# Compressing the paged cache: the next unit's transposes issued inside this unit's matmuls

## The chip, the cores and the metric

The kernel runs as one program on one core of a Trainium2 chip. The metric is the device time of one execution in microseconds (us). Three executions of the kernel before took 2334.25, 2342.62 and 2344.47 us; the median, 2342.62 us, is the time before. A profile of a further execution is what the rows below come from.

## The reference

The reference is one inference step of a two-layer decoder for a prompt of 1024 tokens and for eight decode rows that each have 8192 past tokens in a paged cache. In each layer a normalised input is projected into the inputs of four head groups (sparse attention, a gated recurrence, pooling, attention on a memory), their outputs are gated and projected back. The part that matters here is the sparse attention's compressed keys and values of the decode rows:

```
def compress_rows(rows, pe, w1, w2):          # rows: 8192 cache rows of 64 numbers, keys or values
    blk = rows.reshape(B, n, 32, Hk, 64) + pe # blocks of 32 rows
    flat = blk ... reshape(B, n, Hk, 32 * 64) # 2048 numbers for each block
    return silu(flat @ w1) @ w2               # w1: 2048 x 256, w2: 256 x 64
```

It is done for the keys and for the values of all eight decode rows, 256 blocks each, in both layers; the compressed rows are then what the decode rows score to choose the blocks that they attend to.

## The kernel before

Each layer runs in four phases: A (norms, first projections), P2 (the rest of the projections, prompt attention), P3 (the recurrence, the decode rows' window and memory attention, and the compression of the cache, which is `stageC`), and O (output projection, and the decode rows' selection, which reads the compressed rows). The order of the instructions on each engine is fixed when the program is built: a planner goes through all instructions of a phase by priority and by its own estimate of when each can start, and puts on an engine the first one by priority that is ready by that estimate (L1797). Earlier code has the earlier priority; `stageC` has a later priority than all else in P3 (L1750), so that its matmuls fill what the recurrence and the attention (below: the other lane) leave of TensorE. On the chip every engine keeps that order, whatever the real durations are.

`stageC` (L450) works through 16 units; a unit is 128 blocks, half of a decode row's cache. For each unit:

- `cload` (L511) brings the unit's cache pages into four groups of tiles R (g = 0 to 3), each with two halves. One half comes by four direct DMAs, two issued by SP and two by ACT (L541), the other by two indirect DMAs issued by POOL (L524); one VectorE copy per half (L544) puts the values next to the keys. There are four slots for each half (`rb` is 4), so one unit's rows fill them all, and a group's load can start when the transposes of the group that was there are done.
- `ctrans` (L548) turns R into X, with the positions along the partitions: for each group and for t = 0 (keys) and t = 1 (values), four 128 x 128 transposes on TensorE (L246, tile `ct`) fill one PSUM bank, ACT copies the bank as the rounded part Xh (L564) and VectorE subtracts it for the remainder Xl (L565). The transposes turn through three PSUM banks, which the transposes of the hidden layer (`ct` from `xs`, in `csilu`) use too. X has three buffers for the two sets that a unit needs, so the next unit's key set goes into the free one, and its value set into the one that this unit's key product has done with.
- `cmm` (L568) makes the product with w1 for keys or for values: 16 steps q of three matmuls of 256 columns each (`mm3`, L118: Xh with w1's rounded part, Xh with its remainder, Xl with its rounded part), accumulated in one PSUM bank.
- `ctail` (L612) applies the SiLU and w2 to the unit before, and writes it out (L621, L622, SP).

The order before is: loads of unit u+1; all 48 matmuls of the key product of u; tail of u-1; all 32 transposes of u+1, group by group, keys and values in turn; the 48 matmuls of the value product of u.

Of the kernel before, what the change touches and what calls it, by code (L numbers as in the profile page):

```python
# [9 lines left out]
F32 = mybir.dt.float32  # L10
F32R = mybir.dt.float32r
# [101 lines left out]
class Net:  # L113
# [336 lines left out]
    def stageC(self, l, cp, rb):  # L450

        nc = self.nc
        xp, self.cxp, self.cxn = cp["s"], [cp[f"X{n}"] for n in range(3)], 0
        R = [self.cload(l, 0, g, cp["R"], rb) for g in range(4)]
        W = self.cweights(l, cp)
        X = self.ctrans(R)
        hid = None
        for u in range(16):
            yield u
            R = [self.cload(l, u + 1, g, cp["R"], rb) for g in range(4)] if u < 15 else None  # L460
            new = [self.cmm(X[0], W, 0)]
            if u:
                self.ctail(l, u - 1, hid, W, xp)
            if R:
                nx = self.ctrans(R)
            new.append(self.cmm(X[1], W, 1))
            hid, X = new, nx
        self.ctail(l, 15, hid, W, xp)

    def cpe(self, l, wp):  # L470
# [74 lines left out]
            parts += [(R[:, pr, c1 - 1:c1 + 1], R[:, pr, c1 + 1:c1 + 3]) for pr in range(2)]  # L545
        return parts

    def ctrans(self, Rs):  # L548
        nc = self.nc
        X = []  # L550
        for t in range(2):
            n = self.cxn % 3
            self.cxn += 1
            pool = self.cxp[n]
            X.append([pool.tile([128, 16, 128], F32R, name=f"X{p}{n}", bufs=1) for p in "hl"])
        for g, R in enumerate(Rs):
            for t in range(2):
                ps = self.psT()
                for pr in range(4):
                    self.tr(ps[:, pr * 128:pr * 128 + 128], R[pr][t].rearrange("p s d -> p (s d)"))  # L560
                pv = ps.rearrange("p (b r) -> p r b", r=16)
                hi = X[t][0][:, :, g * 32:g * 32 + 32]
                lo = X[t][1][:, :, g * 32:g * 32 + 32]
                nc.scalar.copy(hi, pv)  # L564
                nc.vector.tensor_tensor(lo, pv, hi.bitcast(F32), op=OP.subtract)  # L565
        return X

    def cmm(self, X, W, t):  # L568
        ps = self.lane("h")
        for q in range(16):  # L570
            w = W[0][t][q // 8]
            self.mm3(ps[:, :256], X[0][:, q], X[1][:, q], w[0][:, q % 8], w[1][:, q % 8], q == 0, q == 15)
        return ps

    def csilu(self, hid, n, bB, xp):

# [1224 lines left out]
```

## Time and profile before

| | |
|---|---|
| median of three executions | 2342.62 us (2334.25 to 2344.47) |
| profiled execution | 2343.6 us |
| span of its instructions | 2341.8 us |
| TensorE matmul busy | 2048.5 us, 87% |
| VectorE, ACT, POOL busy | 65%, 38%, 32% |
| mean granted clock of TensorE | 0.93 |

The profiled execution's time is its span and 1.8 us around it. Times in the rows are microseconds from the start of the span, unless ns is written. PE is TensorE's matmuls and PEld its weight loads, DVE is VectorE, SPq and ACTq are the issues of DMAs. `ct`, `ch` and `R` are tile names; "L246 PE MATMUL ct<-cst,R" is the transposes of R, "ch<-w1h,Xh" a product with w1. A matmul's duration in a row runs past the start of the next one, since matmuls overlap; what one costs is the distance between two starts.

### The profile page before, as it was taken

The numbers are of one execution on the slowest core, as the hardware profiler recorded it, in microseconds if no ns is written. First come the engines' busy times: TensorE is split into PE (matmuls) and PEld (weight loads), VectorE is DVE, ScalarE is ACT, GpSimd is POOL, SyncE is SP. The second block draws the span as 40 slices with busy tenths as digits, with TensorE's granted clock in tenths as the row PEclk, the third lists the DMA queues.
The fourth block names the chain that finished last, engine by engine and source line by source line (L and its number), as shares of the span: only waits on it lengthen the run. The fifth ranks groups of instructions, "written<-read, shape, count | busy, mean of one in ns | idle before, by whom it ended". The sixth has DMA issues, their size and how long they took to land.

```text
span 2341.8 us, 41952 instructions
## 1 busy us (share of the span) xinstructions
PE 2048.5 (87%) x14396; PEld 1824.7 (78%) x14396; DVE 1511.6 (65%) x3927; ACT 888.2 (38%) x2221; POOL 746.7 (32%) x841
## 2 busy tenths in 40 slices
PE   4999998894798999896979999898949899998878
PEld 4997888784788888785669979887838888878645
DVE  7874377885777666553298724788867776656523
ACT  4223366553433323230152234675545333333101
POOL 2002123313655543223020012243146555532340
PEclk8999999997899899898989999999969998998889
DMA  7237321106655446776253363221086544467661
GB/s 249 92 109 184 94 78 52 58 26 169 176 146 149 119 125 184 201 235 200 87 171 105 112 155 98 66 61 47 28 208 170 140 135 136 138 190 221 174 206 51
DMA packets 324093, 312.97 MB, mean 134 GB/s; under 512 B 60619, under 2 KB 285783, under 8 KB 323608
## 3 DMA queue, kind: packets, MB, share of 16 engines
q1 hardware_dynamic: 261544, 213.25, 31.1%
q0 software_dynamic: 24320, 79.71, 11.7%
q10 hardware_dynamic: 38016, 17.32, 2.8%
q8 instruction: 115, 1.88, 0.3%
q14 instruction: 98, 0.80, 0.1%
HBM read 255.00 MB, written 59.57 MB: 134 GB/s over the span
## 4 chain that ended last, share of the span: by engine, by line
PE 58%; DVE 16%; DMA 11%; issue 8%; ACT 3%; POOL 2%; SPq 2%; ACTq 0%; DVEq 0%; another core or an unknown queue 0%; POOLq 0%
PE ch L120 3%; PE ch L122 3%; PE mt L246 3%; PE ct L246 3%; PE ch L121 3%; PE aa L121 3%; PE aa L122 3%; PE aa L120 3%; PE mt L1429 2%; PE oa L122 2%; PE oa L120 2%; PE oa L121 2%; DVE P L804 2%; PE fa L120 2%; PE fa L122 2%
## 5 line engine op out<-in xcount | busy, mean ns | idle before, releaser
L524 POOL DMA_INDIRECT R<-in_cache_nsa_dram,idxc x256 | 253.1, 989 | 295.8 <-PE ct L246 192.5
L120 PE MATMUL ch<-w1h,Xh 128*128 128x256 f32 x1024 | 314.3, 307 | 17.6 <-ACT Xh L564 8.7
L122 PE MATMUL ch<-w1h,Xl 128*128 128x256 f32 x1024 | 311.4, 304 | 6.1 <-DVE Xl L565 3.2
L121 PE MATMUL ch<-w1l,Xh 128*128 128x256 f32 x1024 | 308.7, 301 | 0.4 <-issue 0.4
L120 PEld LDWEIGHTS ch<-w1h,Xh 128*128 128x128 f32 x1024 | 209.1, 204 | 23.5 <-ACT Xh L564 10.2
L122 PEld LDWEIGHTS ch<-w1h,Xl 128*128 128x128 f32 x1024 | 208.4, 204 | 13.8 <-DVE Xl L565 5.7
L148 POOL TENSOR_TENSOR wl<-wf,wh 128x1024 fp32r<-128x1024 f32 (+2 forms) x42 | 94.9, 2271 | 377.1 <-ACT wh L139 295.6
L564 ACT CAST Xh<-ct 128x512 fp32r<-128x512 f32 x256 | 146.0, 585 | 180.0 <-PE ct L246 109.9
L121 PEld LDWEIGHTS ch<-w1l,Xh 128*128 128x128 f32 x1024 | 209.0, 204 | 2.0 <-issue 0.4
L565 DVE TENSOR_TENSOR Xl<-ct,Xh 128x512 fp32r<-128x512 f32 x256 | 172.4, 683 | 42.8 <-ACT Xh L564 26.1
L246 PE MATMUL ct<-cst,R 128*128 128x128 f32 x1024 | 163.9, 292 | 40.7 <-DVE Xl L565 31.0
L246 PEld LDWEIGHTS ct<-cst,R 128*128 128x128 f32 x1024 | 122.1, 149 | 53.2 <-DVE Xl L565 33.7
L544 DVE COPY R<-R 128x256 f32<-128x256 f32 x260 | 92.5, 370 | 107.5 <-DMA R<-in_cache_nsa_dram,idxc 68.9
L121 PE MATMUL aa<-wl,hTh 128*128 128x326 f32 (+1 forms) x512 | 156.6, 307 | 5.1 <-POOL wl L148 5.1
L120 PE MATMUL aa<-wh,hTh 128*128 128x326 f32 (+1 forms) x512 | 156.4, 307 | 4.0 <-ACT wh L139 4.0
L122 PE MATMUL aa<-wh,hTl 128*128 128x326 f32 (+1 forms) x512 | 156.1, 305 | 0.0
L447 ACT ACTIVATE P<-ms,nst 128x512 f32<-128x512 f32 (+3 forms) x192 | 106.6, 557 | 78.7 <-DVE nst L777 78.0
L120 PE MATMUL fa<-hTh,wh 128*128 128x344 f32 x384 | 129.4, 337 | 4.2 <-ACT fo L381 3.9
L122 PE MATMUL fa<-hTh,wl 128*128 128x344 f32 x384 | 125.1, 326 | 0.0
L121 PE MATMUL fa<-hTl,wh 128*128 128x344 f32 x384 | 125.1, 326 | 0.0
L820 DVE TENSOR_TENSOR pl<-mt,ph 128x512 fp32r<-128x512 f32 (+1 forms) x160 | 101.2, 644 | 33.9 <-ACT ph L819 29.0
L777 DVE TENSOR_REDUCE nst<-ms 128x1 f32<-128x512 f32 (+3 forms) x192 | 98.0, 517 | 32.4 <-PE ms L774 19.2
(558 smaller groups left out, 5722.9 us busy)
## 6 DMA issues: line engine op xcount, KB each, us to landing
wf<-in_w_in_dram SPq DMA_DIRECT2D x34, 512.0 KB
R<-in_cache_nsa_dram SPq DMA_DIRECT2D x256, 64.0 KB
R<-in_cache_nsa_dram ACTq DMA_DIRECT2D x256, 64.0 KB
zd<-fo SPq DMA_DIRECT2D x48, 172.0 KB
pwf<-in_cmp_w_dram SPq DMA_DIRECT2D x32, 256.0 KB
wof<-in_w_out_dram SPq DMA_DIRECT2D x16, 512.0 KB
oo<-od SPq DMA_DIRECT2D x16, 512.0 KB
oz<-zd SPq DMA_DIRECT2D x16, 512.0 KB
```

The lines of the kernel that those rows point to most:

```text
L120: mm(out, lh, rh, start=first, stop=False)
L121: mm(out, lh, rl, start=False, stop=False)
L122: mm(out, ll, rh, start=False, stop=last)
L148: e.tensor_tensor(lo, src, hi.bitcast(F32), op=OP.subtract)
L246: self.nc.tensor.transpose(out, in_, self.ident[:in_.shape[0], :in_.shape[0]])
L447: self.nc.scalar.activation(out, S, AF.Exp, bias=nm, accum_out=sm)
L524: nc.gpsimd.indirect_dma_start(R[:, j].rearrange("p c d -> p (c d)"), None, rows, bass.IndirectOffsetOnAxis(ap=self.idxc[:, l, at + j:at + ...
L544: nc.vector.tensor_copy(Rs[:, :, :, 2], R[:, :, 0:2])
L564: nc.scalar.copy(hi, pv)
L565: nc.vector.tensor_tensor(lo, pv, hi.bitcast(F32), op=OP.subtract)
L777: nc.vector.tensor_reduce(one(nm), S, axis=AX.X, op=OP.max, negate=True)
L820: nc.vector.tensor_tensor(pl[:, :n], ps[:, :n], ph[:, :n].bitcast(F32), op=OP.subtract)
```

## The change

The value and key transposes of unit u+1 are no longer one block between the two products of unit u. Each product's loop over q issues the four transposes of one group after steps q = 1, 5, 9 and 13: in the key product those of the keys of u+1, in the value product those of its values. The loads start one unit earlier in the code (unit 1 is loaded before the loop), and the load of group g of unit u+2 stands right behind the value transposes of group g of u+1, in the value product of u. The number of loads, transposes, matmuls, copies and subtracts is the same, and so are the buffers.

```diff
-        R = [self.cload(l, 0, g, cp["R"], rb) for g in range(4)]
+        load = lambda u, g: self.cload(l, u, g, cp["R"], rb)
+        R = [load(0, g) for g in range(4)]
         W = self.cweights(l, cp)
-        X = self.ctrans(R)
+        X = [self.cX() for _ in range(2)]
+        for g in range(4):
+            for t in range(2):
+                self.ctrans(R[g], g, t, X[t])
+        R = [load(1, g) for g in range(4)]
         hid = None
         for u in range(16):
             yield u
-            R = [self.cload(l, u + 1, g, cp["R"], rb) for g in range(4)] if u < 15 else None
-            new = [self.cmm(X[0], W, 0)]
-            if u:
-                self.ctail(l, u - 1, hid, W, xp)
-            if R:
-                nx = self.ctrans(R)
-            new.append(self.cmm(X[1], W, 1))
-            hid, X = new, nx
+
+            new, nx, nR = [], [], []
+            for t in range(2):
+                if u < 15:
+                    nx.append(self.cX())
+                ps = self.lane("h")
+                for q in range(16):
+                    self.cmm(ps, X[t], W, t, q)
+                    if q % 4 == 1 and u < 15:
+                        self.ctrans(R[q // 4], q // 4, t, nx[t])
+                        if t and u < 14:
+                            nR.append(load(u + 2, q // 4))
+                new.append(ps)
+                if t == 0 and u:
+                    self.ctail(l, u - 1, hid, W, xp)
+            hid, X, R = new, nx, nR
...
-    def ctrans(self, Rs):
...
+    def cX(self):
+        n = self.cxn % 3
+        self.cxn += 1
+        return [self.cxp[n].tile([128, 16, 128], F32R, name=f"X{p}{n}", bufs=1) for p in "hl"]
+
+    def ctrans(self, R, g, t, X):
+
+        nc = self.nc
+        ps = self.psT()
+        for pr in range(4):
+            self.tr(ps[:, pr * 128:pr * 128 + 128], R[pr][t].rearrange("p s d -> p (s d)"))
+        pv = ps.rearrange("p (b r) -> p r b", r=16)
+        hi = X[0][:, :, g * 32:g * 32 + 32]
+        lo = X[1][:, :, g * 32:g * 32 + 32]
+        nc.scalar.copy(hi, pv)
+        nc.vector.tensor_tensor(lo, pv, hi.bitcast(F32), op=OP.subtract)
+
+    def cmm(self, ps, X, W, t, q):
+        w = W[0][t][q // 8]
+        self.mm3(ps[:, :256], X[0][:, q], X[1][:, q], w[0][:, q % 8], w[1][:, q % 8], q == 0, q == 15)
```

## Rows read from the trace of the kernel before

**Rows 1.** The profile's page: engines' busy time, and the drains of the transposes.
```profile
PE 2048.5 (87%) x14396; PEld 1824.7 (78%) x14396; DVE 1511.6 (65%) x3927; ACT 888.2 (38%) x2221; POOL 746.7 (32%) x841
L564 ACT CAST Xh<-ct 128x512 fp32r<-128x512 f32 x256 | 146.0, 585 | 180.0 <-PE ct L246 109.9
L565 DVE TENSOR_TENSOR Xl<-ct,Xh 128x512 fp32r<-128x512 f32 x256 | 172.4, 683 | 42.8 <-ACT Xh L564 26.1
```

**Rows 2.** Stage C by layer: PE, PEld, DVE, ACT, POOL busy; clock, DMA share, GB/s.
```profile
598.00:1048.00 450.00, 413.16 (x3412) 374.46 (x3411) 292.42 (x744) 153.08 (x403) 202.62 (x280) 0.93 0.58 166
1750.00:2195.00 445.00, 402.96 (x3361) 367.38 (x3360) 302.13 (x746) 161.97 (x410) 217.96 (x282) 0.91 0.58 163
```

**Rows 3.** Waits of TensorE in layer 0's stretch: total us, times, longest.
```profile
PE ct L246 <- DVE Xl L565: 10.2, 7, 3.6
PE ch L122 <- DVE Xl L565: 3.2, 4, 1.6
PE ch L122 <- DVE R L544: 1.6, 1, 1.6
```

**Rows 4.** The same in layer 1's stretch.
```profile
PE ct L246 <- DVE Xl L565: 9.7, 8, 3.2
PE ch L120 <- ACT Xh L564: 8.7, 3, 6.2
```

**Rows 5.** TensorE in order of time: eight and four transposes among products.
```profile
721.17 1.09 PE L246 MATMUL ct<-cst,R 128*128 128x128 f32 x8
...
722.22 0.28 PE L120 MATMUL ch<-w1h,Xh 128*128 128x256 f32 x1
722.34 0.28 PE L121 MATMUL ch<-w1l,Xh 128*128 128x256 f32 x1
...
723.66 0.60 PE L246 MATMUL ct<-cst,R 128*128 128x128 f32 x4
...
724.21 0.28 PE L121 MATMUL ch<-w1l,Xh 128*128 128x256 f32 x1
```

**Rows 6.** One wait of the transposes, TensorE in order of time.
```profile
758.59 0.63 PE L246 MATMUL ct<-cst,R 128*128 128x128 f32 x4 [2.53 <-DVE Xl L565]
```

**Rows 7.** Busy time and clock just after that wait, and in a longer stretch.
```profile
760.70:767.50 6.80, 6.80 (x43) 6.21 (x44) 4.86 (x13) 1.02 (x3) 0.95 (x2) 0.50 0.55 155
832.40:955.20 122.80, 115.76 (x995) 103.03 (x993) 73.28 (x199) 38.17 (x92) 51.08 (x64) 1.00 0.59 170
```

**Rows 8.** One group's load: transposes that free it, POOL's issue, copies, next transposes.
```profile
776.63 1.06 PE L246 MATMUL ct<-cst,R 128*128 128x128 f32 x8
...
778.45 1.06 POOL L524 DMA_INDIRECT R<-in_cache_nsa_dram,idxc  x1 [0.15 <-issue]
...
784.60 0.53 DVE L544 COPY R<-R 128x256 f32<-128x256 f32 x2 [1.89 <-DMA R<-in_cache_nsa_dram,idxc]
...
809.06 0.62 PE L246 MATMUL ct<-cst,R 128*128 128x128 f32 x4
```

**Rows 9.** First and last product with w1 in each layer.
```profile
L120 PE MATMUL ch<-w1h,Xh x512: 274/283/584, 598.0 to 1020.2; 128*128 128x256 f32 x171
L120 PE MATMUL ch<-w1h,Xh x512: 276/283/582, 1755.1 to 2167.3; 128*128 128x256 f32 x171
```

**Rows 10.** SP's queue in order of time: two stretches of other loads before R's.
```profile
901.14 8.18 SPq L968 DMA_DIRECT2D W<-in_cache_nsa_win_dram  x8
910.11 5.91 SPq L541 DMA_DIRECT2D R<-in_cache_nsa_dram  x4
...
943.23 9.48 SPq L1183 DMA_DIRECT2D msV<-in_cache_mem_dram  x7
...
956.31 0.64 SPq L541 DMA_DIRECT2D R<-in_cache_nsa_dram  x2
```

**Rows 11.** VectorE's longest waits in layer 0's stretch: total us, times, longest.
```profile
DVE R L544 <- DMA R<-in_cache_nsa_dram,idxc: 39.3, 23, 6.4
```

More of the change, by code (lines that the diff above doesn't have):

```diff
@@ L546, in cload @@
         return parts
-    def ctrans(self, Rs):
-        nc = self.nc
[L550 to L573, printed above, removed]
+    def cX(self):
[3 more added lines that the diff above has]
+    def ctrans(self, R, g, t, X):
+        nc = self.nc
+        ps = self.psT()
[9 more added lines that the diff above has]
+        self.mm3(ps[:, :256], X[0][:, q], X[1][:, q], w[0][:, q % 8], w[1][:, q % 8], q == 0, q == 15)
     def csilu(self, hid, n, bB, xp):
```

## The prediction

> **What bounds the kernel now.** I read the busy times first, then the busy times by stretch, then TensorE's waits inside the two stretches that hold stage C, and last the queues that feed it. TensorE is busy 87% of the span and no other engine passes 65% [rows 1]. The change touches only stage C, so its stretches matter: 450 us in layer 0 and 445 us in layer 1 [rows 2]. In them TensorE is busy 413.2 and 403.0 us, that is 92% and 91%, VectorE 65 and 68%. The phase is bound by TensorE, and what a new order can give back is the rest: 36.8 + 42.0 = 78.8 us without a matmul, and what the lower clock takes. The mean granted clock is 0.93 and 0.91 there [rows 2]; since the clock has two levels, 2.4 and 1.2 GHz, the time at the lower one is 2 x 0.07 x 450 + 2 x 0.09 x 445 = 143 us, and work done in it would have taken half: at most 71 us.
>
> The waits tell whose fault the idle time is. Those that belong to the chain from the transposes to the products are transposes that wait for a bank until Xl is out of it (10.2 and 9.7 us), products that wait for Xl, for the copy in R, or for Xh (3.2, 1.6 and 8.7 us): 33.4 us together [rows 3, 4], 42% of the 78.8. The other 45 belong to the recurrence, the hidden layer's chain and the decode rows' attention, which the change leaves alone.
>
> **The transposes themselves: 0.** The number stays. Their cost among products is read from distances between starts [rows 5]: products alone stand 722.34 - 722.22 = 0.12 us apart; eight transposes and one product take 722.22 - 721.17 = 1.05, so the eight take 0.93; four and one product take 0.55, so the four take 0.43. A group of four is not dearer than half of an eight (0.465). A layer has 128 groups, both have 256; were all now in eights the change would gain 256 x 0.035 = 9 us; if each group of four paid a boundary of 0.08 (0.20 instead of 0.12 for the first product behind it, were it not already in the 0.43) for the half of the groups that are new, it would lose 10. I take 0: fours already stand among products in these very rows, because the planner lets value products in while a bank is not free. The change therefore spreads over the key product what is now woven into the value product only.
>
> **The waits for drains: -25.** Now a group is issued as soon as the planner thinks that its bank is free. The drain is ACT's 0.585 and VectorE's 0.683 behind it [rows 1], 1.27 us without the handing over, and anything else that holds VectorE goes straight into a wait of TensorE, as the 2.53 us of [rows 6]. After the change two groups are twelve products and four transposes apart, 12 x 0.12 + 0.43 = 1.87 us. With three banks a bank comes round after two whole distances and twelve products, 2 x 1.87 + 1.44 = 5.2 us, against 1.27: some 3.9 us in hand. The longest waits for Xl are 3.6 and 3.2 us [rows 3, 4], so most would go. So would the products' waits: the key set is complete half a unit before its product, and the value set has a whole key product between its last group and its own product. But the hidden layer's transposes take two turns of the same three banks in each unit, and the planner need not keep the even order that the code writes. Between 0 and -33.4 I take three quarters.
>
> **The clock: -11.** Behind the wait of [rows 6] the clock is 0.50 for 6.8 us with TensorE busy all through [rows 7]: 3.4 us lost for a gap of 2.5. If the 71 us were shared as the idle time is, 42% or 30 us would go with the 33.4; since part of the low time is itself idle, and other gaps next to the removed ones hold the clock down, I take half of three quarters of that. Bounds 0 and -30.
>
> **The loads: +10.** This is where the change takes something away. A slot of R is now freed by the value transposes and refilled long before it is wanted: the transposes that free one end at 777.7, POOL issues at 778.45, the copies end at 785.1, and the next transposes come at 809.06 [rows 8]. That is 7.4 us of load and 24 us in hand. After the change a group is held from its key transposes to its value transposes, half a unit later, and the load has the other half. A unit lasts (1020.2 - 598.0) / 16 = 26.4 us in layer 0 and 25.8 in layer 1 [rows 9], so the half is 13.2 and what is left in hand is 5.8 us. POOL's two issues per group fit, and so do ACT's. SP is the queue to look at: it issues two of a group's six DMAs and is at times taken by other loads for longer, 9.0 us from 901.14 to 910.11 and 13.1 from 943.23 to 956.31 [rows 10]; there are six such stretches, three in each layer (the recurrence's first loads, the window's, the memory's). Over 5.8 that leaves 3.2 and 7.3, on average 5.2, and a fall of the clock of 3.4 each: 6 x 8.6 = 51 us if nothing else covers it. What covers it are the products: with a group late, the rest of the key product, 48 x 0.12 = 5.8 us, and the value product can go first, if the planner has foreseen it. Bounds 0 and 51; I take a fifth, because the planner sees these loads stand in SP's queue and only misjudges how long they take.
>
> Here the Trainium skill speaks to a term. Its page "DMA: Bandwidth & Descriptors", section "Issuing engines are not separate DMA queues", says that issuing from several engines saves only the time on the sequencer, and that this time is usually small beside the transfer. By that rule SP's turn would not delay a load, the term would be nought and the sum 2307. The row disagrees: eight issues took SP 8.18 us [rows 10], more than a whole load of 7.4. I go by the row.
>
> **The rest: 0.** The prologue makes the same transposes and loads in the same order. At the end, unit 15's last group stands near the end of unit 14's value product, a few microseconds before R goes to the output phase, which has all of unit 15's products to wait for anyway. Give 5 us either way for a new order of the other lane, whose instructions still go first by priority.
>
> **Sum.** -25 - 11 + 10 = -26 on the profiled execution's 2343.6 us: 2317.6. That execution is 1.0 above the median of the runs, so on the median 2317 us.
>
> **Rivals.** First, that nothing much changes. The planner issues by readiness and had woven fours into the value products already [rows 5]; it may fill its own plan to the brim either way, and the waits come from what it misjudges, so that they turn up at other instructions. For it: 45 of the 78.8 us of idle time have nothing to do with transposes. Against it: the waits for Xl recur, fifteen times. Time 2343, within 8.
>
> Second, slower: the loads become the bound. The place is the key transposes of unit u+1 in the key product of u, the point is when load and queue together pass 13.2 us, and the price is the 51 us above. VectorE keeps its order too, and it waits 39.3 us for indirect loads in layer 0 already [rows 11]; a copy that waits longer holds up the Xl behind it, which takes half of the gain (36) away: 2343.6 + 51 - 18 = 2376, and between that and about 2352 if half of the six stretches bite. For it: 24 us in hand shrink to 5.8. Against it: that is still more than the usual lateness, 39.3 / 23 = 1.7 us.
>
> Third, slower: the clock. Products that alternate with transposes all through a unit change banks all the time and may stop for moments at each change; if the low time then doubled with the woven share, 143 us more at half rate cost 71, less the 25: 2390. Against it: 122.8 us in a row, with transposes among the value products in several units, ran at 1.00 [rows 7]. The Trainium skill has this as a rule: "TensorE: Matmul & The Clock Gate", section "A second HAM failure mode: psum-queue depth-cycling", tells of a kernel whose cycling through banks made TensorE idle for moments and its clock swing. By that rule the time is the 2390; the trace speaks against it.
>
> **Chances.** Forecast 0.50, with its own range 2298 to 2333; nothing changes 0.23; loads 0.21; clock 0.04; 0.02 for what I don't see. For the range I go down to 2290 (a third more than my gain, most of the bounds of the drain and clock terms) and up to 2364, the middle of the loads' case. What a measurement of this kernel can tell from no change is about 0.5%, 12 us. Faster by more holds nearly all of the forecast and a fifth of the first rival, 0.55; within it 0.21; slower 0.24.
>
> **What would show it.** Transposes of R in fours with about twelve products between them through the whole unit, in the key product too. Waits of transposes for Xl under 7 us in both layers together, waits of products for Xl and Xh near none; the mean clock 0.94 or more in both stretches; both stretches some 13 us shorter; from the end of a group's copies to its key transposes some 6 us instead of 24. I am wrong if transposes or copies of R wait for DMAs by tens of microseconds, if the key product is still solid, or if the stretches are shorter and the output phase gives it back.

## The result, and the profile after

The changed kernel takes 2397.8 us (2396.3 to 2400.0), the kernel before 2339.9 beside it: ratio 1.0249, 95% interval 1.0223 to 1.0276. It is slower, and outside the range that was given. Two later timings gave 1.0205 [1.0154, 1.0257] and 1.0225 [1.0202, 1.0249]. The kernel before itself took 2274 to 2276 us beside some of the experiments and 2340 to 2345 beside the others, so only ratios to it are compared.

The profiled execution took 2398.2 us (span 2396.3). First the page's busy times and drains, which answer to [rows 1], then the busy times of the two stretches [rows 2] and the first and last product of stage C in each layer [rows 9].

```profile
PE 2078.7 (87%) x14396; PEld 1845.2 (77%) x14396; DVE 1509.4 (63%) x3927; ACT 887.3 (37%) x2221; POOL 735.7 (31%) x841
L575 ACT CAST Xh<-ct 128x512 fp32r<-128x512 f32 x256 | 147.8, 584 | 336.9 <-PE ct L246 211.9
L576 DVE TENSOR_TENSOR Xl<-ct,Xh 128x512 fp32r<-128x512 f32 x256 | 173.8, 684 | 59.3 <-ACT Xh L575 45.0
```

```profile
598.00:1058.00 460.00, 408.93 (x3320) 369.95 (x3321) 275.07 (x726) 143.95 (x392) 203.66 (x280) 0.90 0.52 147
1780.00:2240.00 460.00, 406.66 (x3333) 368.12 (x3334) 289.54 (x741) 156.06 (x404) 207.13 (x282) 0.91 0.54 151
```

```profile
L120 PE MATMUL ch<-w1h,Xh x512: 274/283/582, 596.8 to 1051.0; 128*128 128x256 f32 x171
...
L120 PE MATMUL ch<-w1h,Xh x512: 277/283/581, 1784.9 to 2233.2; 128*128 128x256 f32 x171
```

The drains did not get dearer: they last 584 and 684 ns, as before. ScalarE waits longer for the transposes (211.9 us instead of 109.9). From its first to its last product stage C lasts 454.2 us instead of 422.2 and 448.3 instead of 412.2: 68 us more. Between the two stages stand 734 us instead of 735, and behind the second one 163.1 instead of 174.5. So stage C loses all of it, and the end gives 11 back. TensorE's records between first and last product, added up, split the 68: 32 us are time without a matmul (35.0 to 49.7 and 32.8 to 49.9), 24 are half of the longer busy time at the lower clock (148 us of it instead of 100), and 12 are more busy time at full clock. Only some 3 of these 12 are other work, 32 matmuls of the memory attention that came to lie inside layer 1's stage; the rest are longer distances between starts, 6 us of them at the first product of a step.

The clock fell in both layers. In layer 0 it went from 0.93 to 0.90. In layer 1 the two figures of 0.91, here and in [rows 2], hide it, because both stretches run past the last product. Between first and last product it is 0.93 before, in the first line, and 0.91 after, in the second:

```profile
1755.10:2167.30 412.20, 379.36 (x3261) 347.81 (x3260) 279.91 (x724) 150.18 (x393) 196.65 (x268) 0.93 0.57 162
1784.90:2233.20 448.30, 398.36 (x3294) 362.28 (x3295) 278.58 (x726) 147.80 (x393) 204.10 (x281) 0.91 0.53 147
```

What TensorE waits for, layer 0's stretch and then layer 1's, answers to [rows 3, 4]: total us, times, longest.

```profile
PE ct L246 <- DVE R L557: 12.4, 8, 4.5
...
PE ct L246 <- issue: 7.8, 3, 5.3
...
PE ct L246 <- DVE Xl L576: 2.9, 4, 1.0
```

```profile
PE ct L246 <- issue: 13.2, 6, 5.3
PE ct L246 <- DVE Xl L576: 8.9, 9, 3.3
PE ct L246 <- DVE R L557: 7.5, 3, 5.5
```

The waits for drains are indeed smaller. Of the 33.4 us that the prediction priced, 27.8 lie between first and last product, and 7.0 of these are left, 3.2 in layer 0 and 3.8 in layer 1. The other 5.6 stand in the prologue of layer 1, which the change leaves alone, as do 5.1 of the 8.9 in layer 1's rows. The transposes now wait for the copies inside the loaded rows R, which they never did between first and last product before. Most of what is listed as "issue" there is the same wait: in front of each of the longest ones a copy of R ended 0.10 us before. With these it is 20 us in layer 0 and 19 in layer 1.

The next rows follow one group of the changed kernel as [rows 8] do before: the value transposes that free the slot, POOL's and SP's issues, the last copy, the key transposes, the value transposes.

```profile
899.64 0.60 PE L246 MATMUL ct<-cst,R 128*128 128x128 f32 x4
...
903.66 0.95 POOL L537 DMA_INDIRECT R<-in_cache_nsa_dram,idxc  x1 [0.30 <-issue]
...
906.65 3.12 SPq L554 DMA_DIRECT2D R<-in_cache_nsa_dram  x3
...
911.48 0.29 DVE L557 COPY R<-R 128x256 f32<-128x256 f32 x1 [0.82 <-DMA R<-in_cache_nsa_dram]
...
911.83 1.11 PE L246 MATMUL ct<-cst,R 128*128 128x128 f32 x4 [0.58 <-DVE R L557]
...
924.28 0.60 PE L246 MATMUL ct<-cst,R 128*128 128x128 f32 x4
```

The slot is free at 900.2 and the copy ends at 911.8, 11.5 us instead of 7.4; TensorE takes the keys as soon as they are there, and the values 12.4 us later. The same four distances, taken over the 56 groups of a layer that are loaded inside the loop (us, layer 0 / layer 1; "late" counts groups whose copy ended under 1.5 us ahead of their transposes, with an error of two or three because copies can change places):

```
                          slot free to copied  copied to keys  keys to values  late of 56
kernel before                  10.3 / 10.3       14.9 / 14.4      1.6 /  1.7     0 /  0
change                         12.0 / 12.1        2.5 /  2.6     14.9 / 14.3    23 / 18
values only                     9.3 /  9.8       16.3 / 14.8      1.4 /  1.4     0 /  0
half hold                      11.7 / 11.8        2.8 /  2.6     13.3 / 12.2    21 / 25
five slots                     11.4 / 10.9       10.3 / 10.6     12.4 / 13.0     5 /  3
four slots, same cuts           9.7 / 10.4        4.8 /  4.4     12.7 / 13.5     9 /  8
five slots, other cuts         10.1 / 11.0        7.1 /  7.2     14.6 / 14.0    10 /  8
four slots, other cuts         11.2 / 11.1        1.4 /  1.6     14.0 / 13.9    32 / 28
the same, timed again          12.0 / 11.7        2.1 /  2.1     13.3 / 13.1    25 / 21
```

The longest waits come where the memory attention's rows are loaded. SP's queue, ScalarE, VectorE and TensorE of the changed kernel in order of time, and then busy times in the 40 us from SP's burst on in both layers (columns as in [rows 2]):

```profile
951.45 8.52 SPq L1190 DMA_DIRECT2D msV<-in_cache_mem_dram  x7
...
952.70 1.07 ACT L575 CAST Xh<-ct 128x512 fp32r<-128x512 f32 x2 [2.52 <-PE ct L246]
...
956.00 0.70 DVE L557 COPY R<-R 128x256 f32<-128x256 f32 x2 [6.65 <-DMA R<-in_cache_nsa_dram,idxc]
...
956.80 1.08 PE L246 MATMUL ct<-cst,R 128*128 128x128 f32 x4 [5.26 <-issue]
...
957.09 1.27 DVE L576 TENSOR_TENSOR Xl<-ct,Xh 128x512 fp32r<-128x512 f32 x2
...
965.28 3.28 SPq L554 DMA_DIRECT2D R<-in_cache_nsa_dram  x3
...
970.04 1.09 PE L246 MATMUL ct<-cst,R 128*128 128x128 f32 x4 [4.49 <-DVE R L557]
```

```profile
951.00:991.00 40.00, 26.95 (x170) 25.20 (x169) 20.76 (x44) 7.69 (x17) 10.14 (x11) 0.74 0.74 232
2129.00:2169.00 40.00, 26.26 (x165) 23.85 (x163) 20.35 (x43) 6.79 (x17) 9.19 (x10) 0.74 0.76 232
```

And the kernel before, from its burst on:

```profile
943.00:983.00 40.00, 30.89 (x225) 28.38 (x225) 24.04 (x52) 11.63 (x26) 16.02 (x16) 0.87 0.90 260
2112.00:2152.00 40.00, 31.37 (x250) 29.88 (x248) 24.76 (x51) 12.00 (x28) 7.58 (x8) 0.87 0.65 193
```

335 matmuls instead of 475 fit into these 80 us. At the 3412 in 450 us of [rows 2] the missing 140 are worth an estimated 18 us: about a quarter of the 68. The rest is spread over other units, which last from 7 us less to 11 us more than before.

The same rows show what a copy does that VectorE reaches too early. ScalarE had copied two banks by 953.8, but VectorE stood for a load until 956.0 and subtracted the two banks only from 957.1 on: two finished drains waited 3.3 us behind a copy.

### The profile page after: what moved, and what is told of

Read it like the earlier page. It is cut to its first block, busy times and chain, and to the rows that moved or that the text cites. A ratio compares the mean times of both kernels' runs of the same rounds, so it can differ in the third digit from the quotient of the medians.

```text
span 2396.3 us, 41986 instructions
## 1 busy us (share of the span) xinstructions
PE 2078.7 (87%) x14396; PEld 1845.2 (77%) x14396; DVE 1509.4 (63%) x3927; ACT 887.3 (37%) x2221; POOL 735.7 (31%) x841
## 4 chain that ended last, share of the span: by engine, by line
PE 58%; DVE 14%; DMA 10%; issue 8%; ACT 4%; POOL 2%; SPq 2%; another core or an unknown queue 1%; ACTq 0%; DVEq 0%; POOLq 0%
PE ct L246 4%; PE ch L120 4%; PE ch L122 4%; PE ch L121 4%; PE mt L246 3%; PE aa L121 3%; PE aa L120 3%; PE aa L122 3%; PE mt L1436 3%; PE oa L121 2%; PE oa L122 2%; PE oa L120 2%; DVE P L811 2%; DMA R<-in_cache_nsa_dram 2%; PE fa L120 2%
## 5 line engine op out<-in xcount | busy, mean ns | idle before, releaser
L120 PE MATMUL ch<-w1h,Xh 128*128 128x256 f32 x1024 | 324.3, 317 | 6.8 <-issue 3.9
L575 ACT CAST Xh<-ct 128x512 fp32r<-128x512 f32 x256 | 147.8, 584 | 336.9 <-PE ct L246 211.9
L246 PE MATMUL ct<-cst,R 128*128 128x128 f32 x1024 | 185.3, 303 | 69.8 <-issue 23.9
L122 PEld LDWEIGHTS ch<-w1h,Xl 128*128 128x128 f32 x1024 | 212.1, 207 | 12.6 <-issue 10.3
L246 PEld LDWEIGHTS ct<-cst,R 128*128 128x128 f32 x1024 | 129.9, 154 | 83.8 <-issue 43.9
L557 DVE COPY R<-R 128x256 f32<-128x256 f32 x260 | 85.3, 345 | 90.5 <-DMA R<-in_cache_nsa_dram,idxc 54.2
```

The source lines that it names most:

```text
L120: mm(out, lh, rh, start=first, stop=False)
L122: mm(out, ll, rh, start=False, stop=last)
L246: self.nc.tensor.transpose(out, in_, self.ident[:in_.shape[0], :in_.shape[0]])
L557: nc.vector.tensor_copy(Rs[:, :, :, 2], R[:, :, 0:2])
```

## The experiments

Each is timed beside the kernel before. The cuts shown leave out lines, marked with dots, that only carry the edit through. The runs follow in the order in which they were made. The kernel before was at 2274 us beside the first four (values only to no loads) and at 2276 beside another four (from the cuts in the values-only order to the extra transposes), and at 2343 to 2345 beside all others.

**Values only.** All eight groups of a unit stand in the value product, the load right behind: the weave without the hold.

```diff
-                if u < 15:
-                    nx.append(self.cX())
+                if t and u < 15:
+                    nx = [self.cX() for _ in range(2)]
...
-                    if q % 4 == 1 and u < 15:
-                        self.ctrans(R[q // 4], q // 4, t, nx[t])
-                        if t and u < 14:
+                    if t and q % 4 == 1 and u < 15:
+                        for s in range(2):
+                            self.ctrans(R[q // 4], q // 4, s, nx[s])
+                        if u < 14:
```

> Both sets of transposes of a group stand in the value product, after steps 1, 5, 9 and 13, and the load right behind them: the groups are spread by hand as in the change, but a slot of R is held no longer than before. If the loss comes from slots held half a unit longer: the loads have some 24 us again, about 2340, between 2325 and 2350. If the spreading itself costs (clock, boundaries, a worse plan): most of the loss stays, 2370 to 2400.

Measured 2281.4 us, ratio 1.0022 [0.9998, 1.0046]. The loss is gone, and so are the waits for R; transposes wait for Xl again (17.2 us in layer 0). The change itself was not timed while the kernel before took 2274 us; the late-loads run below has this order too and gives 1.0036 where the change gives 1.0205.

**Half hold.** Key groups behind steps 8, 10, 12, 14 of the key product, value groups behind 0, 2, 4, 6 of the value product.

```diff
-                    if q % 4 == 1 and u < 15:
-                        self.ctrans(R[q // 4], q // 4, t, nx[t])
+                    g = q // 2 - (0 if t else 4)
+                    if q % 2 == 0 and 0 <= g < 4 and u < 15:
+                        self.ctrans(R[g], g, t, nx[t])
...
-                            nR.append(load(u + 2, q // 4))
+                            nR.append(load(u + 2, g))
```

> As the change, but the key transposes stand after steps 8, 10, 12 and 14 of the key product and the value transposes after steps 0, 2, 4 and 6 of the value product, so that a slot is held for 8 steps instead of 16: the load has three quarters of a unit, 20 us, 12 in hand instead of 6. If the hold is the cause: 2340 to 2360, at least half of the loss gone. If the weave is the cause, which is the same in number and denser: 2390 or more.

Measured 2308.6 us, ratio 1.0186 [1.0135, 1.0237]: a miss. But the table shows why: the planner placed the groups so that the slots were still held 13.3 and 12.2 us. The edit did not do what it was for.

**No loads.** The loads and copies of units 2 to 15 are left out, and unit 1's rows are used for all of them: in the change, whose edit is shown, and in the kernel before.

```diff
-                            nR.append(load(u + 2, q // 4))
+                            nR.append(R[q // 4])
```

> The change without the loads and copies of R for units 2 to 15 (unit 1's rows are used again, so the compressed rows are of the wrong units). If late loads are the cause, the change's order is no slower than the order before under the same cut: within 12 us of the next run, and both some 20 to 60 us below 2340. If the weave is the cause: 40 to 60 us above the next run.

> The kernel before with the same loads and copies left out (unit 1's rows are used again, so the compressed rows are of the wrong units): the partner of the run above. Both theories: 2290 to 2325, since the transposes' waits for drains stay and VectorE has 0.37 us less per copy to do.

Measured 2181.8 us, ratio 0.9589 [0.9569, 0.9609], and 2171.4 us, ratio 0.9547 [0.9531, 0.9563]. The distance of the two is within what was expected, their fall is not: 93 and 103 us below the 2274 beside them, where 20 to 60 and 15 to 50 below 2340 had been expected. Stage C's stretches, first of the change and then of the kernel before, both without loads:

```profile
590.00:956.00 366.00, 358.32 (x3293) 334.94 (x3292) 244.13 (x611) 145.58 (x389) 96.15 (x168) 0.98 0.22 65
1669.00:2040.00 371.00, 362.55 (x3303) 336.63 (x3304) 255.25 (x619) 157.45 (x399) 96.77 (x169) 0.98 0.24 66
```

```profile
593.00:964.00 371.00, 361.03 (x3311) 333.90 (x3310) 253.48 (x617) 145.55 (x396) 96.69 (x168) 0.99 0.24 69
1666.00:2040.00 374.00, 363.92 (x3315) 337.03 (x3314) 262.26 (x625) 154.01 (x403) 97.68 (x168) 0.98 0.24 69
```

Without loads TensorE is busy 97 to 98% in either order and its clock is 0.98 or 0.99. So the drains and banks, which the change was to relieve, cost next to nothing by themselves: the idle time and the low clock of stage C come with the loads and their copies, which this pair does not tell apart. The change is then even 4.4 and 2.3 us shorter inside stage C, but what follows each stage is 11 us longer, and in sum it is 10 us slower. Loads cost 4.5% in the old order.

**Late loads.** Values only, with the loads issued in the key product of the next unit.

```diff
+                    if t == 0 and q % 4 == 1 and 0 < u < 15:
+                        R.append(load(u + 1, q // 4))
...
-                        if u < 14:
-                            nR.append(load(u + 2, q // 4))
```

> The values-only order (all eight groups woven into the value product, ratio 1.002 before), but the loads of the next unit are issued in the key product, half a unit later than there, so a load has the same 13.2 us before its transposes as in the change, and nothing is held longer than in the kernel before. Theory A (what costs is how little time a load is given before its transposes): the loss comes back, ratio 1.020 (1.012 to 1.030), and the transposes of stage C wait for copies of R by 8 us or more per layer. Rival C (what costs is the splitting into keys with keys and values with values, or the longer hold by itself, whatever time the load has): ratio 1.002 (0.998 to 1.006) and waits for R under 3 us per layer.

Measured 2354.9 us, ratio 1.0036 [1.0010, 1.0063]. That would speak against theory A, but the trace shows that nothing moved: the planner issues a load as soon as its slot is free, wherever it is written. From slot free to copied it is 9.5 us in layer 0, from copied to keys 16.1. It is the values-only order once more, and told nothing of the slack.

**Late copies, values only.** Each copy is bound, on VectorE, behind the drain of a later group.

```diff
-            nc.vector.tensor_copy(Rs[:, :, :, 2], R[:, :, 0:2])
+            copy = lambda Rs=Rs, R=R: nc.vector.tensor_copy(Rs[:, :, :, 2], R[:, :, 0:2])
+            copy() if late is None else late.append(copy)
...
+                        for _ in range((2 * (u > 0), 2 * (u > 0), 0, 4 * (u < 14))[q // 4]):
+                            with self.tc.issue_after(x):
+                                late.pop(0)()
```

> The values-only order, with the same loads at the same places, but each copy of a loaded row on VectorE is queued behind the drain of a later group (10, 7, 20 and 20 us behind its load instead of where the order put it, at about the time the load lands). Theory B (VectorE stands in the copies, 138 us of waits for the loads' DMAs in the values-only run, and the drains queued behind it make TensorE wait for Xl, 24 and 17 us in the two layers' stages): the waits of the copies fall under 30 us, the waits for Xl under 8 us per layer, and the ratio goes to 0.985 (0.975 to 0.993), faster than both kernels. Rival (VectorE's waits fill time that it had; TensorE's waits for Xl come from the drains' own length): ratio 1.002 (0.997 to 1.006), Xl waits within 30% of where they were.

Measured 2317.2 us, ratio 0.9869 [0.9829, 0.9909]: faster than both kernels, as theory B expected. VectorE's waits in the copies, over the whole run: first the late-loads run, which was timed beside it and has the same order, then this one.

```profile
DVE R L558 <- DMA R<-in_cache_nsa_dram,idxc: 88.9, 55, 6.1
...
DVE R L558 <- DMA R<-in_cache_nsa_dram: 17.5, 15, 4.0
```

```profile
DVE R L561 <- DMA R<-in_cache_nsa_dram,idxc: 6.8, 2, 6.5
DVE R L561 <- DMA R<-in_cache_nsa_dram: 6.7, 6, 2.6
```

TensorE's waits for Xl fell from 12.0 and 13.8 us in the two layers' stretches to 5.7 and 3.4. The two stages together are 48 us shorter than in the late-loads run, 40 of them in layer 1, and 11 come back around them. Layer 1's stretch of the late-loads run, and of this one.

```profile
1758.00:2193.00 435.00, 387.87 (x3298) 354.81 (x3299) 282.91 (x728) 153.43 (x394) 203.02 (x281) 0.92 0.57 155
```

```profile
1750.00:2147.00 397.00, 368.14 (x3271) 336.99 (x3269) 285.77 (x727) 155.07 (x400) 203.15 (x271) 0.97 0.61 170
```

A copy that stands on VectorE for a load holds up the drains behind it, as at 956.00 above, and these hold up TensorE. 10 of 56 groups have their copy late now, and transposes wait 13 us for such copies, so this version can still be mended.

**Late copies in the change.** The same, each copy behind the drain three groups later.

```diff
+                        for _ in range(2 if late and (q > 12 if t else q < 12) else 0):
+                            with self.tc.issue_after(x):
+                                late.pop(0)()
```

> The change itself, with each copy of a loaded row queued on VectorE behind the drain three groups later (about 10 us behind its load, 3 us ahead of its key transposes). Theory A (the transposes wait for late loads, VectorE's standing is a symptom): the ratio stays at 1.020 to 1.030 and the transposes still wait 15 us or more per layer for R. Theory B (VectorE stands in copies for which the load is not there yet, and the drains of the group before are queued behind it): the ratio falls to 1.000 (0.990 to 1.010), waits for R under 8 us per layer.

Measured 2444.8 us, ratio 1.0392 [1.0342, 1.0441]: worse than either theory said. The copies end 16.9 us after the slot is free, 1.0 us ahead of the keys, and 39 of 56 groups are late. By the order that the edit sets, each copy now waits for a drain, that drain for its transposes, and these for their copy: a chain through three engines. There was no room to put the copy later.

**The change again**, unaltered, beside these three.

> The change unaltered, beside the three others on one chip. By every theory the same ratio as measured before, 1.025 (1.020 to 1.030), since none rests on the chip; a ratio under 1.015 would say that the loss hangs on how fast this chip's transfers or clock are.

Measured 2402.2 us, ratio 1.0205 [1.0154, 1.0257].

**Five slots, and four with the same cuts.** A fifth slot needs room; it comes from single buffers in the units' tails and from one buffer less of two tiles of the recurrence. The four-slot run has the same cuts without the first line.

```diff
-                    for u in self.stageC(l, cp, 4):
+                    for u in self.stageC(l, cp, 5):
...
+        nb = 2 if bB is None else 1
...
-            xs = xp.tile([128, 256], F32, name="xs", bufs=2)
-            th = xp.tile([128, 256], F32, name="xth", bufs=2)
+            xs = xp.tile([128, 256], F32, name="xs", bufs=nb)
+            th = xp.tile([128, 256], F32, name="xth", bufs=nb)
...
-            E = t1("hE", 4)
-            x = t1("hKQ", 5)
+            E = t1("hE", 3)
+            x = t1("hKQ", 4)
```

> The change with five slots for loaded rows in the place of four; the room comes from single buffers for xs, xth, ko and vo and one buffer less of hE and hKQ. Theory A (a slot of R goes round once per unit: 12 us from being free to the copy's end, and in the change 14.5 us from the key transposes to the value transposes in place of 1.6, together 26.5 us of a unit's 27, so that about 20 of 56 groups have their copy less than 1.5 us ahead of their transposes, none before): a fifth slot gives each round a quarter more, the groups that are late fall under 8 of 56 per layer, the waits for R under 6 us per layer, and the ratio falls to 1.002 (0.990 to 1.010). Rival C (the splitting into keys with keys and values with values costs by its order alone): within 0.5% of the same cuts with four slots.

> The change with the same smaller buffers, but four slots: what the cuts themselves cost. By every theory about the change's own ratio, 1.022 (1.012 to 1.035), with some 20 of 56 groups late and a round of 30 us.

Measured 2379.9 us, ratio 1.0158 [1.0125, 1.0192], and 2382.5 us, 1.0170 [1.0139, 1.0202]. Slots are free in time with five (5 and 3 late groups), and the time is the same: a miss for theory A. But the pair tests little, because the smaller buffers alone had taken most of the waits for R away: 8 us of them in both layers with four slots and 3 with five, against 39 in the change. So the cuts say more than the fifth slot: with 31 us of these waits less, the ratio is 1.0170 where the change's is 1.0205 to 1.0249. Layer 0's waits, of five slots and then of four:

```profile
PE ct L246 <- DVE Xl L576: 13.2, 13, 4.4
...
PE ch L614 <- ACT hh L601: 4.1, 2, 3.7
...
PE ch L121 <- DVE hl L602: 3.7, 3, 3.1
...
PE ct L246 <- DVE R L557: 0.3, 1, 0.3
```

```profile
PE ch L120 <- DVE xs L594: 7.3, 6, 3.3
PE ct L246 <- DVE Xl L576: 5.7, 8, 1.7
PE ct L246 <- DVE R L557: 5.5, 3, 2.7
```

Part of what R no longer costs, the drains and the tails take.

**Values only, held.** One extra transpose per group, whose result is not used, reads the slot half a unit later, and the load follows it.

```diff
+                    if t == 0 and q % 4 == 1 and 0 < u < 15:
+                        with self.tc.issue_after(self.nc.cur_bb.bb.instructions[-1]):
+                            self.tr(self.psT()[:, :128], held[q // 4][0][0].rearrange("p s d -> p (s d)"))
+                        R.append(load(u + 1, q // 4))
...
-            hid, X, R = new, nx, nR
+            hid, X, held, R = new, nx, R, nR
```

> The values-only order (ratio 1.002), in which each slot of R is held for half a unit more by one extra transpose that reads it in the next unit's key product (nothing uses its result; 56 of them per layer, at 0.11 us some 12 us or 0.5% in all), and its load follows that transpose. Nothing is woven into the key product otherwise. Theory A (the round of the slot): ratio 1.022 (1.010 to 1.035) with 15 or more of 56 groups late per layer. Rival C (the order of the change): 1.006 (1.002 to 1.010), and no more than 5 groups late.

Measured 2385.2 us, ratio 1.0189 [1.0150, 1.0228]. Transposes wait for R 11.9 and 12.8 us per layer, none did in the values-only run. It looked like theory A, until the control below.

**Five slots with late copies**, each behind the drain two groups later, with the cuts of the first five-slot run.

```diff
+                        for _ in range(2 if late and (q > 8 if t else q < 8) else 0):
+                            with self.tc.issue_after(x):
+                                late.pop(0)()
```

> The change with five slots and the same cuts, and each copy queued on VectorE behind the drain two groups after its load (some 7 us). Theories A and B together (no slot late any more, and VectorE no longer standing in copies): ratio 0.985 (0.972 to 0.995), faster than the kernel before and about as fast as the values-only order with late copies. Rival: the copies behind the drains make the transposes late again, as in the change with late copies: 1.01 to 1.04.

Measured 2351.5 us, ratio 1.0049 [1.0026, 1.0071]: 1.1% better than five slots alone, but not faster than the kernel before, and short of the 0.985 expected. VectorE's waits in the copies for loads fell from 104 us to 16. So its standing seems to be paid in this order too.

**The cuts in the values-only order.** The same smaller buffers, four slots.

> The values-only order (1.002), four slots, with the cuts of the five-slot run (single buffers for xs, xth, ko and vo, one buffer less of hE and hKQ). Theory A (the round of the slot; the cuts hid the fifth slot's gain by new waits of the units' tails, some 14 us per layer for xs, hh and hl): ratio 1.012 (1.006 to 1.018) without a late group. Rival C (the cuts cost nothing, the order of the change costs all): 1.002 (0.998 to 1.005).

Measured 2279.6 us, ratio 1.0016 [0.9984, 1.0048]: the cuts cost nothing there. In the change's order their partner is the four-slot run above.

**Other cuts, five slots and four.** The room comes from the recurrence alone; each buffer has one less.

```diff
-            E = t1("hE", 4)
-            x = t1("hKQ", 5)
+            E = t1("hE", 3)
+            x = t1("hKQ", 4)
...
-        D = t1("hD")
+        D = t1("hD", 1)
...
-        oc = t1("hoc")
+        oc = t1("hoc", 1)
```

> The change with five slots, the room taken from the recurrence's buffers alone (one less each of hKQ, hE, hoc and hD), so that the units' tails keep theirs. Theory A: fewer than 8 of 56 groups late, waits for R under 5 us per layer, no new waits for xs, hh or hl, ratio 1.003 (0.993 to 1.009). Rival C (keys with keys and values with values cost by their order): 1.015 to 1.022, as in the first five-slot run.

> The change with four slots and the same cuts of the recurrence's buffers: their own cost. By both theories 1.022 (1.012 to 1.032), with 15 or more of 56 groups late per layer; if it comes near the five-slot run, the fifth slot does nothing.

Measured 2286.4 us, 1.0041 [1.0010, 1.0071], and 2283.8 us, 1.0021 [0.9992, 1.0049]. Again the fifth slot brought nothing in sum. In the profiled executions it did shorten stage C (805.5 us of both layers instead of 837.3), while what lies around was 16 us longer; but of the ten executions with four slots the profiled one is the longest, 2295.9 us. And four slots, with more late groups than the change itself, lost nothing. Layer 0's waits of that run:

```profile
PE ct L246 <- DVE R L557: 18.9, 10, 9.1
PE ct L246 <- DVE Xl L576: 6.3, 7, 1.6
```

With 2.2 us that are listed as "issue", and 14.6 in layer 1, that is 36 us of waits for R in this longest execution, nearly the change's 39, at 0.9% above the kernel before. Beside 2276 us, then, such waits do not cost what the change lost beside 2343.

**Extra transposes only**, at the places of the held run, but reading a constant; nothing is held. The cut is against the held run.

```diff
-                            self.tr(self.psT()[:, :128], held[q // 4][0][0].rearrange("p s d -> p (s d)"))
-                        R.append(load(u + 1, q // 4))
+                            self.tr(self.psT()[:, :128], self.ident)
```

> The values-only order with the same number of extra transposes at the same places as the held run (1.019), but reading a constant, so that no slot is held and the loads follow the value transposes as in the values-only order. Theory A: 1.005 (1.001 to 1.009), the extra transposes alone; the held run's other 1.4% is the hold. Rival (the extra transposes and the banks that they take cost it): 1.015 or more.

Measured 2318.2 us, ratio 1.0172 [1.0111, 1.0234], where theory A said 1.005. The extra transposes cost all that the held run lost, and the hold no amount that shows. The waits for Xl were 32 us in layer 1's stretch here and 15 in the values-only run; in layer 0's they were 24 in both.

**The change and the four-slot run on one chip.**

> The change unaltered, a third time, beside the four-slot run with one buffer less each of hKQ, hE, hoc and hD (1.002 on another chip than the change has been timed on). Theory X (how much room the recurrence's buffers give the other streams decides: with full buffers they run ahead and take VectorE's, ScalarE's and the queues' time between a load and its transposes): the change 1.022 (1.012 to 1.032) on this chip too. Theory Y (it is the chip): the change within 0.6% of the four-slot run beside it.

> The change with four slots and one buffer less each of hKQ, hE, hoc and hD, again. Theory X: 1.002 (0.996 to 1.008) on this chip too, stage C 418 us per layer instead of 450. Theory Y: within 0.6% of the unaltered change beside it.

Measured 2395.5 us, 1.0225 [1.0202, 1.0249], and 2372.9 us, 1.0143 [1.0096, 1.0189]. Between the theories: the smaller buffers take 0.8% off, and the remaining 1.2% between 1.0143 and 1.0021 go with the time that the kernel before took beside them (2343 and 2276). Stage C's stretches, of the change and of the four-slot run:

```profile
597.00:1054.00 457.00, 407.28 (x3311) 369.25 (x3312) 272.84 (x726) 145.78 (x394) 203.92 (x281) 0.90 0.52 148
1780.00:2237.00 457.00, 403.28 (x3311) 366.55 (x3311) 281.44 (x733) 152.23 (x401) 202.51 (x281) 0.90 0.53 148
```

```profile
600.00:1035.00 435.00, 380.36 (x3261) 345.90 (x3261) 273.72 (x718) 144.68 (x389) 201.87 (x273) 0.93 0.53 154
1776.00:2205.00 429.00, 385.27 (x3299) 352.64 (x3299) 279.57 (x730) 152.69 (x399) 205.04 (x281) 0.93 0.57 159
```

The four-slot run's clock is 0.93 in both, the change's 0.90. Its slots are as full, but its transposes wait less for R: 23 us over both stretches, with those listed as "issue", against 44 in the change. Here the 21 us of waits and the 22.6 us of time nearly agree.

## Why the prediction was wrong

**The step that failed first is "The loads: +10".** Its working was "7.4 us of load and 24 us in hand", and "what is left in hand is 5.8". One chain had been taken for all [rows 8]. Over all groups it is 10.3 us from slot free to copied in the kernel before, and 12.0 in the change; what was left in hand was 2.5. The mean hides the queues: in the change's layer 0 SP, in [rows 8] not looked at, makes a group's last issue 5.9 us after the slot is free, ScalarE 3.8 and POOL 4.1. By the ratios, loads take 1.0225 - 0.9589 = 6.4% of the time in the change and 4.5% in the kernel before: the term is 1.8%, 43 us, inside its bounds of 0 and 51 and four times the value taken. With the change's other two ratios it is 38 or 48 us. The change was timed beside the kernel before at 2343 us and the runs without loads beside it at 2274, so the 43 carries that error. The term had counted SP's bursts alone; by the estimate above they are 18 of it, and the rest stands elsewhere.

**"The waits for drains: -25" was right as a count and wrong as a gain.** The waits for Xl and Xh fell nearly as forecast, by 20.8 us between first and last product. But the change without loads is 10 us slower, not 36 faster: with no load in the way, 6.5 us of these waits are left in the old order too. So most of them came with the loads, and not from banks that come round too early. VectorE, which stands in its copies for the loads [rows 11], is the likely cause: late copies brought 1.1 and 1.7% in the two orders in which there was room. In the order before they were not tried. Of the 81 us between forecast and result, some 46 are this gain that did not come, with the clock's, and some 33 are the loads.

**"The clock: -11" had the wrong sign.** It went with the idle time, as assumed, and that grew: 24 us lost. The 78.8 us of idle time and the 143 us at the lower clock, from which it was worked out, were too large: their stretches run some 28 us past the last product of each layer, and between first and last product it is 67.8 and 117.

**SP's bursts** were priced as six stretches of 8.6 us. Two were found to bite, both at the memory's loads, at 18 us together by the matmuls that did not fit. The loads of R behind them were issued 18 to 21 us after their slots were free. But the row that the prediction set against a rule was misread. A merged row of SP's queue runs from its first issue to the end of its last, with the waits between them: in the 8.52 us at 951.45 the seven issues take 3.5, 0.37 to 0.93 each, and in the 8.18 us of [rows 10] the eight take 5.7. The longest wait within the 8.52 is for another load, issued at 947.76, that landed at 955.25:

```profile
SPq L1190 <- DMA msq<-qmd: 2.9, 1, 2.9
```

The Trainium skill ("DMA: Bandwidth & Descriptors", "Issuing engines are not separate DMA queues") has it that the time to issue is usually small beside the transfer. This trace agrees: an issue takes 0.37 to 0.93 us here, and that load took 7.5 to land. SP was late all the same, since its queue stood for earlier transfers.

**"The transposes themselves: 0" and "The rest: 0"** stand as far as was seen: without loads stage C is 4.4 and 2.3 us shorter. But what follows each stage is 11 us longer there, and in the change the end is 11 us shorter; why is not known. The prediction had 5 either way.

**The range.** Its lower end, 2290, was called a third more than the gain; it is twice the gain of 26 us. The result lies above the upper end, so this did not matter.

**The rivals.** The clock's, 2390, came nearest in number, 8 us short, by luck: without loads the products alternate with transposes all through and the clock is 0.98, so its mechanism does not explain the result. "The loads become the bound", 2376, was 22 us short; its chance was 0.21. Its remark that a longer wait of a copy holds up the Xl behind it was the better half of the explanation, and it was left a remark.

**What is shown, and what stays open.** Shown: most of the loss needs the loads (1.8 of 2.2%; 0.4%, or 10 us, is left without them), by the profiles it lies in stage C, and with all groups in the value product all but 0.2 to 0.4% of it is gone. Shown in part: putting the copies behind later drains brought 1.1 and 1.7% and took VectorE's waits in them away; the edit moves other instructions of the plan too, so the price of the standing alone is not known. Not shown, though it was my theory for most of the runs: that the hold of the slots is the price. The hold makes transposes wait for R, 39 us of it. But with smaller buffers 8 us of these waits were left and the loss was still 1.7%, a fifth slot brought nothing in either pair, and one run with 36 us of such waits lost little. Against that stands the last pair, in which the waits fell by 21 us and the time by 23. So the waits are a part of the price at most. What else in the order of keys with keys and values with values costs the 1 to 2% is open. Other lanes' work that stands in the way may have a share, since one buffer less of four of the recurrence's tiles gave 0.8% back. The change itself was never timed while the kernel before took 2276 us, so how much of its loss hangs on that is open too.

## What to carry to other kernels

Before a buffer is held longer, measure over all its rounds, not in one, the time from when it is free to when its data can be used, with every queue and copy in it. Where an engine that works in order also copies loaded data into place, bind that copy behind work that comes later than the load, if there is room: it gained 1.7 and 1.1% here in two orders, and cost 1.9% in the change itself, where there was none. And when a full buffer is found behind a loss, give it room before calling it the cause: here most of the waits went, and most of the loss stayed. And take a merged row of a queue apart into its issues and its waits before calling it the time of the issues.

## What the runs showed of the hardware

One transpose more per group, 0.11 us of TensorE each among products at full clock and some 12 us in all, cost 1.5% (1.0172 against 1.0022), nearly three times that. None of them waited, so the rest came up elsewhere. Each takes a turn of the three banks as well; that this is the reason is not shown, since the waits for Xl rose in layer 1 only.

The kernel before took 2274 us and later 2345 on one and the same chip, in all its executions each time. The values-only order was profiled beside both (the values-only and the late-loads run). Between the two stages, the same work took 706 us beside the first and 728 beside the second, with TensorE equally busy. What differed is not known. First the one, then the other:

```profile
1020.00:1726.00 706.00, 626.78 (x3890) 549.84 (x3888) 466.90 (x1230) 293.95 (x713) 161.38 (x137) 0.95 0.42 121
```

```profile
1028.00:1756.00 728.00, 626.61 (x3882) 549.57 (x3880) 466.80 (x1229) 293.10 (x716) 162.84 (x137) 0.93 0.39 116
```
